# RMSNorm and SiLU over 8192 rows: loads move to ScalarE's queue, stores to SyncE's, and two of four rows are squared on each engine

## The chip, the cores and the metric

The kernel runs on one core of one Trainium2 chip. The metric is device time in microseconds (us), as the median of several executions; one further execution was recorded by the profiler. The engines that matter here are VectorE (DVE in the profile), ScalarE (ACT), SyncE (SP, which here only issues transfers) and the 16 DMA engines that move data between the chip's memory (HBM) and the on-chip buffer (SBUF). A transfer is issued by an instruction on an engine's instruction queue; in the profile ACTq and SPq are the queues of ScalarE and SyncE.

## The reference

```python
batch, seq_len, hidden = 8, 1024, 2048      # x is float32, 67.1 MB
rms = np.sqrt(np.mean(x ** 2, axis=-1, keepdims=True) + eps)
out = gamma * x / rms
return (out * (1 / (1 + np.exp(-out)))).astype(np.float32)
```

Each of the 8192 rows of 2048 numbers is divided by its root mean square, multiplied by gamma, and passed through SiLU. All of x is read once and an output of the same size is written once.

## The kernel before

The rows are cut into 16 blocks of 512 rows. A block is one SBUF tile `xt` of 128 partitions with four rows of 2048 float32 in each (4.194 MB), and it is worked on in place. Six such tiles exist (`BUFS`), so block b uses the tile of block b - 6.

For a block b the work is:

- `load(b)` (line 53): one DMA into the tile, issued on SyncE's queue.
- `sums(b)`: the sum of squares of each of the four rows. VectorE does some rows (line 65), ScalarE the others with a Square that accumulates (line 69). `na` (line 63) is the number of rows for ScalarE: three in blocks 2 to 14, two in the others. Then ScalarE takes the root (line 75), for which it loads another function table, and loads the Silu table back.
- `invert(b)`: VectorE's reciprocal (line 80).
- `finish(b)`: four VectorE instructions (line 85), one for each row, multiply by the reciprocal and by gamma; then ScalarE does one Silu over the whole block (line 89). In the last block (`halves`) the Silu and the store come by halves, two rows each.
- `store(b)` (line 94): one DMA out, issued on ScalarE's queue, followed by the issue of `load(b + 6)` on SyncE's queue, which has to wait until that store has landed, since it overwrites the tile.

The order on each engine is the order of the calls, written out by hand. In the loop (lines 127 to 130) `sums(b + 1)` comes ahead of `finish(b)`. The store of block b - 1 stands behind the first Square of block b + 1 on ScalarE (`after_first`), and that Square waits for block b + 1 to land.

At the start five loads are issued, VectorE fills `ones` by 32 small memsets, gamma comes in by a small DMA on ScalarE's queue into a tile of the same pool (`grow`, line 103), TensorE spreads it over all partitions into PSUM (line 114), and 16 copies (line 117) bring it to SBUF as `g`. The sixth load (line 118) takes the tile that held gamma.

Of the kernel before, what the change touches and what calls it, by code (L numbers as in the profile page):

```python
# [1 line left out]

# [4 lines left out]

ACT = mybir.ActivationFunctionType
ALU = mybir.AluOpType


@with_exitstack
def kernel(
    ctx: ExitStack,
    tc: tile.TileContext,
    x: bass.AP,
    gamma: bass.AP,
    eps: bass.AP,
    out: bass.AP,
):  # L20

    nc = tc.nc
    P = nc.NUM_PARTITIONS
    f32 = mybir.dt.float32
    x2 = x.flatten_outer_dims()  # L30
    o2 = out.flatten_outer_dims()
    n, d = x2.shape
    J = 4
    BUFS, LEAD = 6, 6
    nblk = n // (P * J)
    xb = x2.rearrange("(b p j) d -> b p (j d)", p=P, j=J)
    ob = o2.rearrange("(b p j) d -> b p (j d)", p=P, j=J)

    singles = ctx.enter_context(tc.tile_pool(name="singles", bufs=1))
    pool = ctx.enter_context(tc.tile_pool(name="pool", bufs=BUFS))  # L40
    small = ctx.enter_context(tc.tile_pool(name="small", bufs=2))
    psum = ctx.enter_context(tc.tile_pool(name="psum", bufs=1, space=bass.MemoryType.PSUM))

    g = singles.tile([P, d], f32)
    eps_t = singles.tile([P, 1], f32)
    ones = singles.tile([P, P], f32)
    junk_a = psum.tile([P, d], f32, name="junk_a")
    junk_v = psum.tile([P, d], f32, name="junk_v")
    blocks, rmss, rstds = {}, {}, {}

    def load(b):
        xt = pool.tile([P, J * d], f32, name="xt")
        nc.sync.dma_start(out=xt, in_=xb[b])
        blocks[b] = xt

    def row(b, j):
        return blocks[b][:, j * d:(j + 1) * d]

    def sums(b, after_first=()):


        ss = small.tile([P, J], f32, name="ss")
        na = J - 1 if 2 <= b <= 14 else J // 2
        for j in range(na, J):
            nc.vector.tensor_tensor_reduce(  # L65
                out=junk_v, in0=row(b, j), in1=row(b, j), scale=1.0, scalar=0.0,
                op0=ALU.mult, op1=ALU.add, accum_out=ss[:, j:j + 1])
        for j in range(na):
            nc.scalar.activation(out=junk_a, in_=row(b, j), func=ACT.Square,  # L69
                                 accum_out=ss[:, j:j + 1])  # L70
            if j == 0:
                for s in after_first:
                    store(s)
        rms = small.tile([P, J], f32, name="rms")
        nc.scalar.activation(out=rms, in_=ss, func=ACT.Sqrt, scale=1.0 / d, bias=eps_t)  # L75
        rmss[b] = rms

    def invert(b):
        rstd = small.tile([P, J], f32, name="rstd")
        nc.vector.reciprocal(out=rstd, in_=rmss.pop(b))  # L80
        rstds[b] = rstd

    def finish(b, halves=False):
        for j in range(J):
            nc.vector.scalar_tensor_tensor(out=row(b, j), in0=row(b, j), scalar=rstds[b][:, j:j + 1],  # L85
                                           in1=g, op0=ALU.mult, op1=ALU.mult)
            if j % 2 and (halves or j == J - 1):
                cols = slice((j - 1) * d, (j + 1) * d) if halves else slice(0, J * d)
                nc.scalar.activation(out=blocks[b][:, cols], in_=blocks[b][:, cols], func=ACT.Silu)  # L89
                if halves:  # L90
                    nc.scalar.dma_start(out=ob[b][:, cols], in_=blocks[b][:, cols])

    def store(b):
        nc.scalar.dma_start(out=ob[b], in_=blocks[b])
        if b + LEAD < nblk:
            load(b + LEAD)

    with tc.manual_schedule():


        Q = 4
        w = d // Q
        grow = pool.tile([P, J * d], f32, name="xt")
        for b in range(BUFS - 1):
            load(b)
        for c in range(0, P, 4):
            nc.vector.memset(ones[:, c:c + 4], 1.0)  # L107
        nc.vector.memset(eps_t, float(eps))  # L108
        nc.scalar.activation(out=junk_a[:, 0:1], in_=ones[:, 0:1], func=ACT.Square)  # L109
        nc.scalar.dma_start(out=grow[0:P:P // Q, 0:w],  # L110
                            in_=bass.AP(tensor=gamma.tensor, offset=gamma.offset, ap=[[w, Q], [1, w]]))
        for c in range(Q):
            k = c * (P // Q)
            nc.tensor.matmul(junk_v[:, c * w:(c + 1) * w], ones[k:k + 1, :], grow[k:k + 1, 0:w],  # L114
                             start=True, stop=True)
        for c in range(0, d, P):
            nc.vector.tensor_copy(out=g[:, c:c + P], in_=junk_v[:, c:c + P])  # L117
        load(BUFS - 1)


        last = nblk - 1
        sums(0)
        invert(0)
        finish(0)
        sums(1)
        invert(1)
        for b in range(1, last - 1):
            sums(b + 1, after_first=[b - 1])
            finish(b)
            invert(b + 1)  # L130
        store(last - 2)
        finish(last - 1)
        store(last - 1)
        sums(last)
        invert(last)
        finish(last, halves=True)


# [1 line left out]
_INS = ['x', 'gamma', 'eps']  # L140
_OUTS = [((8, 1024, 2048), 'float32')]

_NUMBERS = {'eps': 9.999999747378752e-06}


# [26 lines left out]
```

## Time and profile before

| what | value |
|---|---|
| three runs | 317.79, 319.18, 319.30 us; median 319.18 |
| profiled execution | 319.30 us, of which the profile's span is 317.5 us |
| busy in the span | VectorE 195.0 us (61%), ScalarE 246.6 us (78%), TensorE 2.1 us |
| moved | 67.12 MB read, 67.11 MB written, 423 GB/s over the span |
| loads | 16 of 4096 KB, median 36.2 us from issue to landing |
| stores | 15 of 4096 KB, median 35.7 us; 2 of 2048 KB, 12.7 us |

Some groups of instructions, each with the mean time of one:

| line, engine | what | count | one, ns |
|---|---|---|---|
| L85 DVE | row times reciprocal times gamma, 128 x 2048 | 64 | 2348 |
| L65 DVE | sum of squares, 128 x 2048 | 19 | 2298 |
| L69 ACT | Square with sum, 128 x 2048 | 45 | 1878 |
| L89 ACT | Silu, 128 x 8192 (15) and 128 x 4096 (2) | 17 | 6628 |
| L75 and L89 ACT | table load | 15 and 15 | 1283 |

Times in the profile are counted from the start of the span. A row of the timeline gives start, duration, engine, line, operation, output and input tile, and in brackets how long the engine was idle ahead of it and what it waited for. A row of the stages gives the stretch and its length, the busy time of each engine, the clock granted to TensorE, the busy share of the DMA engines and their rate. A row of waits gives the waiting instruction, what it waited for, and the total, the count and the longest. The time from issue to landing of a transfer includes what it spends queued behind others.

### The profile page before, as it was taken

The page shows a single profiled execution, that of the slowest core. Times are in us where ns is not written, and L with a number is a line of the kernel's source. Part 1 is how long each engine was busy: PE and PEld are TensorE (multiplying, and loading weights), DVE is VectorE, ACT ScalarE, POOL GpSimd, SP SyncE. Part 2 cuts the span into 40 slices and gives each one's busy share as a digit, 9 for nine tenths or more (in the row PEclk, how much of TensorE's full clock was granted, in tenths as well). Part 3 has the DMA queues.
Part 4 walks back from the last instruction along what each step waited for, and adds up shares of the span by engine and source line. Part 5 has one row for each costly group of instructions (what it writes and reads, how often), then busy time and mean ns, then how long its engine had stood idle before and what let it go on. Part 6 is the DMA issues. An engine that isn't in the chain of part 4 may idle for free.

```text
span 317.5 us, 484 instructions
## 1 busy us (share of the span) xinstructions
PE 2.1 (1%) x8; PEld 0.5 (0%) x8; DVE 195.0 (61%) x167; ACT 246.6 (78%) x155; POOL 0.2 (0%) x4
## 2 busy tenths in 40 slices
PE   0200000000000000000000000000000000000000
PEld 0000000000000000000000000000000000000000
DVE  1679279959493918639094490945819369953800
ACT  1352994999999999997896868968689786797620
POOL 0000000000000000000000000000000000000000
DMA  8999999999999999999999999999999999999994
GB/s 331 409 447 438 421 396 413 446 438 421 442 417 451 409 462 405 454 429 429 446 413 462 396 462 409 450 429 429 442 417 458 400 458 425 433 433 430 447 407 208
DMA packets 4764, 134.26 MB, mean 423 GB/s; under 512 B 532, under 2 KB 532, under 8 KB 536
## 3 DMA queue, kind: packets, MB, share of 16 engines
q1 hardware_dynamic: 2304, 67.11, 49.5%
q10 hardware_dynamic: 2456, 67.12, 49.0%
q14 instruction: 4, 0.03, 0.0%
HBM read 67.12 MB, written 67.11 MB: 423 GB/s over the span
## 4 chain that ended last, share of the span: by engine, by line
DMA 49%; ACT 22%; DVE 17%; issue 7%; DVEq 1%; PE 1%; ACTq 0%; SPq 0%
DMA out_dram<-xt 24%; DMA xt<-in_x_dram 23%; ACT xt L89 14%; DVE xt L85 13%; ACT junk_a L69 4%; DMA xt<-in_gamma_dram 2%; DVE junk_v L65 2%; ACT L75 2%; ACT L89 1%; DVE g L117 1%; DVEq L167 1%; PE junk_v L114 1%; ACT rms L75 0%; DVE rstd L80 0%; DVE ss L65 0%
## 5 line engine op out<-in xcount | busy, mean ns | idle before, releaser
L85 DVE SCALAR_TENSOR_TENSOR xt<-xt,rstd,g 128x2048 f32<-128x2048 f32 x64 | 146.2, 2348 | 0.1
L89 ACT ACTIVATE xt<-xt 128x8192 f32<-128x8192 f32 (+1 forms) x17 | 112.7, 6628 | 36.1 <-DVE xt L85 36.0
L69 ACT ACTIVATE junk_a<-xt 128x2048 f32<-128x2048 f32 x45 | 84.5, 1878 | 18.3 <-DMA xt<-in_x_dram 16.7
L65 DVE CUSTOM_DVE_ANT_0 junk_v<-xt 128x2048 f32<-128x2048 f32 x19 | 43.7, 2298 | 60.9 <-DMA xt<-in_x_dram 60.8
L80 DVE RECIPROCAL rstd<-rms 128x4 f32<-128x4 f32 x16 | 2.8, 175 | 34.6 <-ACT rms L75 34.6
L75 ACT ACT_TABLE_LOAD x15 | 19.2, 1283 | 1.5 <-DVE ss L65 1.3
L89 ACT ACT_TABLE_LOAD x15 | 19.2, 1283 | 0.3
L117 DVE COPY g<-junk_v 128x128 f32<-128x128 f32 x16 | 3.3, 281 | 8.6 <-PE junk_v L114 8.6
L69 ACT ACTIVATION_READ_ACCUMULATOR junk_a<-xt 128x1 f32 x45 | 8.4, 186 | 0.0
L75 ACT ACTIVATE rms<-ss,eps_t 128x4 f32<-128x4 f32 x16 | 4.8, 297 | 0.2
L65 DVE DVE_READ_ACCUMULATOR2_ANT ss<- 128x1 f32 x19 | 2.7, 142 | 0.0
L114 PE MATMUL junk_v<-xt,ones 1*128 1x512 f32 x8 | 2.1, 1132 | 8.2 <-DMA xt<-in_gamma_dram 8.2
L109 ACT ACT_TABLE_LOAD x1 | 1.3, 1283 | 0.7 <-PEq L153 0.7
L107 DVE MEMSET ones<- 128x4 f32 x32 | 0.9, 62 | 0.8 <-PEq L153 0.8
L114 PEld LDWEIGHTS junk_v<-xt,ones 1*128 1x128 f32 x8 | 0.5, 305 | 8.2 <-issue 8.2
L109 ACT ACTIVATE junk_a<-ones 128x1 f32<-128x1 f32 x1 | 0.2, 174 | 0.0
L153 POOL MEMSET const-bfloat16-1.0<- 128x1 bf16 x1 | 0.1, 102 | 0.0
L153 POOL MEMSET const-uint8-127<- 128x1 uint8 x1 | 0.1, 101 | 0.0
L153 POOL MEMSET const-float32-0.0<- 128x1 f32 x1 | 0.1, 99 | 0.2 <-issue 0.2
L153 POOL MEMSET const-float32-1.0<- 128x1 f32 x1 | 0.1, 98 | 0.0
L108 DVE MEMSET eps_t<- 128x1 f32 x1 | 0.1, 59 | 0.0
## 6 DMA issues: line engine op xcount, KB each, us to landing
xt<-in_x_dram SPq DMA_DIRECT2D x16, 4096.0 KB, 36.2
out_dram<-xt ACTq DMA_DIRECT2D x15, 4096.0 KB, 35.7
out_dram<-xt ACTq DMA_DIRECT2D x2, 2048.0 KB, 12.7
xt<-in_gamma_dram ACTq DMA_DIRECT2D x1, 8.0 KB
```

Source lines behind the costliest of these rows:

```text
L65: nc.vector.tensor_tensor_reduce(out=junk_v, in0=row(b, j), in1=row(b, j), scale=1.0, scalar=0.0, op0=ALU.mult, op1=ALU.add, accum_out=ss[ ...
L69: nc.scalar.activation(out=junk_a, in_=row(b, j), func=ACT.Square, accum_out=ss[:, j:j + 1])
L75: nc.scalar.activation(out=rms, in_=ss, func=ACT.Sqrt, scale=1.0 / d, bias=eps_t)
L80: nc.vector.reciprocal(out=rstd, in_=rmss.pop(b))
L85: nc.vector.scalar_tensor_tensor(out=row(b, j), in0=row(b, j), scalar=rstds[b][:, j:j + 1], in1=g, op0=ALU.mult, op1=ALU.mult)
L89: nc.scalar.activation(out=blocks[b][:, cols], in_=blocks[b][:, cols], func=ACT.Silu)
L107: nc.vector.memset(ones[:, c:c + 4], 1.0)
L109: nc.scalar.activation(out=junk_a[:, 0:1], in_=ones[:, 0:1], func=ACT.Square)
L114: nc.tensor.matmul(junk_v[:, c * w:(c + 1) * w], ones[k:k + 1, :], grow[k:k + 1, 0:w], start=True, stop=True)
L117: nc.vector.tensor_copy(out=g[:, c:c + P], in_=junk_v[:, c:c + P])
L153: nc = _bacc.Bacc("TRN2", target_bir_lowering=False, num_devices=1)
L167: with _tile.TileContext(nc) as tc:
```

## The change

- Loads are issued on ScalarE's queue. Six are issued at the very start. In the loop `sums(b + 1)` issues `load(b + 3)` behind its first Square, for blocks 6 to 15; the load still has to wait until the store of block b - 3, which used the tile, has landed.
- Stores are issued on SyncE's queue, directly after `finish(b)` in the program. SyncE has nothing else to issue except gamma's small load.
- `na` is two in every block: each engine takes two rows' squares.
- Silu comes by halves of a block in every block, and not only in the last one. The store is still one for a block, except in the last.
- `ones` is filled by one memset, `g` by one copy of 2048 columns, and gamma's row has a tile of its own, so that all six tiles of the pool are free for blocks from the start.

```diff
-    BUFS, LEAD = 6, 6
+    BUFS = 6
...
+    Q = 4
+    w = d // Q
+    grow = singles.tile([P, w], f32)
...
-        nc.sync.dma_start(out=xt, in_=xb[b])
+        nc.scalar.dma_start(out=xt, in_=xb[b])
...
-        na = J - 1 if 2 <= b <= 14 else J // 2
+        na = J // 2
...
             if j == 0:
                 for s in after_first:
-                    store(s)
+                    load(s)
...
-            if j % 2 and (halves or j == J - 1):
-                cols = slice((j - 1) * d, (j + 1) * d) if halves else slice(0, J * d)
+            if j % 2:
+                cols = slice((j - 1) * d, (j + 1) * d)
                 nc.scalar.activation(out=blocks[b][:, cols], in_=blocks[b][:, cols], func=ACT.Silu)
                 if halves:
-                    nc.scalar.dma_start(out=ob[b][:, cols], in_=blocks[b][:, cols])
+                    nc.sync.dma_start(out=ob[b][:, cols], in_=blocks[b][:, cols])

     def store(b):
-        nc.scalar.dma_start(out=ob[b], in_=blocks[b])
-        if b + LEAD < nblk:
-            load(b + LEAD)
+        nc.sync.dma_start(out=ob[b], in_=blocks[b])
...
-        grow = pool.tile([P, J * d], f32, name="xt")
-        for b in range(BUFS - 1):
+        for b in range(BUFS):
             load(b)
-        for c in range(0, P, 4):
-            nc.vector.memset(ones[:, c:c + 4], 1.0)
+        nc.vector.memset(ones, 1.0)
...
-        nc.scalar.dma_start(out=grow[0:P:P // Q, 0:w],
+        nc.sync.dma_start(out=grow[0:P:P // Q, :],
...
-        for c in range(0, d, P):
-            nc.vector.tensor_copy(out=g[:, c:c + P], in_=junk_v[:, c:c + P])
-        load(BUFS - 1)
+        nc.vector.tensor_copy(out=g, in_=junk_v)
...
         finish(0)
+        store(0)
         sums(1)
         invert(1)
         for b in range(1, last - 1):
-            sums(b + 1, after_first=[b - 1])
+            sums(b + 1, after_first=[b + 3] if BUFS <= b + 3 < nblk else [])
             finish(b)
+            store(b)
             invert(b + 1)
-        store(last - 2)
```

More of the change, by code (lines that the diff above doesn't have):

```diff
@@ L86, in finish @@
                                            in1=g, op0=ALU.mult, op1=ALU.mult)
-            if j % 2 and (halves or j == J - 1):
-                cols = slice((j - 1) * d, (j + 1) * d) if halves else slice(0, J * d)
+            if j % 2:
+                cols = slice((j - 1) * d, (j + 1) * d)
                 nc.scalar.activation(out=blocks[b][:, cols], in_=blocks[b][:, cols], func=ACT.Silu)
                 if halves:
-                    nc.scalar.dma_start(out=ob[b][:, cols], in_=blocks[b][:, cols])
+                    nc.sync.dma_start(out=ob[b][:, cols], in_=blocks[b][:, cols])
     def store(b):
-        nc.scalar.dma_start(out=ob[b], in_=blocks[b])
-        if b + LEAD < nblk:
-            load(b + LEAD)
+        nc.sync.dma_start(out=ob[b], in_=blocks[b])
     with tc.manual_schedule():
-        Q = 4
-        w = d // Q
-        grow = pool.tile([P, J * d], f32, name="xt")
-        for b in range(BUFS - 1):
+        for b in range(BUFS):
             load(b)
-        for c in range(0, P, 4):
-            nc.vector.memset(ones[:, c:c + 4], 1.0)
+        nc.vector.memset(ones, 1.0)
         nc.vector.memset(eps_t, float(eps))
         nc.scalar.activation(out=junk_a[:, 0:1], in_=ones[:, 0:1], func=ACT.Square)
-        nc.scalar.dma_start(out=grow[0:P:P // Q, 0:w],
-                            in_=bass.AP(tensor=gamma.tensor, offset=gamma.offset, ap=[[w, Q], [1, w]]))
+        nc.sync.dma_start(out=grow[0:P:P // Q, :],
+                          in_=bass.AP(tensor=gamma.tensor, offset=gamma.offset, ap=[[w, Q], [1, w]]))
         for c in range(Q):
             k = c * (P // Q)
-            nc.tensor.matmul(junk_v[:, c * w:(c + 1) * w], ones[k:k + 1, :], grow[k:k + 1, 0:w],
+            nc.tensor.matmul(junk_v[:, c * w:(c + 1) * w], ones[k:k + 1, :], grow[k:k + 1, :],
                              start=True, stop=True)
-        for c in range(0, d, P):
-            nc.vector.tensor_copy(out=g[:, c:c + P], in_=junk_v[:, c:c + P])
-        load(BUFS - 1)
+        nc.vector.tensor_copy(out=g, in_=junk_v)
         last = nblk - 1
```

## The prediction, made before the changed kernel was run

> **What bounds the kernel now.** I read the page first, its rows of busy DMA and of the DMA queues.
>
> ```profile
> DMA  8999999999999999999999999999999999999994
> GB/s 331 409 447 438 421 396 413 446 438 421 442 417 451 409 462 405 454 429 429 446 413 462 396 462 409 450 429 429 442 417 458 400 458 425 433 433 430 447 407 208
> ...
> q1 hardware_dynamic: 2304, 67.11, 49.5%
> q10 hardware_dynamic: 2456, 67.12, 49.0%
> ```
>
> The two queues (loads on SyncE's, stores on ScalarE's) together keep the 16 DMA engines busy for 98.5% of the span; VectorE has 61% and ScalarE 78%. Next the same by stage; the last two numbers of a line are the DMA share and GB/s, with a packet counted where it starts.
>
> ```profile
> 1.00:1.50 0.50, 0.00 (x0) 0.00 (x0) 0.50 (x20) 0.50 (x1) 0.00 (x0) 1.00 0.00 0
> 1.50:2.00 0.50, 0.00 (x0) 0.00 (x0) 0.26 (x10) 0.50 (x1) 0.00 (x0) 1.00 2.96 786
> 2.00:12.00 10.00, 2.09 (x8) 0.54 (x8) 1.67 (x9) 0.18 (x2) 0.00 (x0) 1.00 0.91 384
> 12.00:40.00 28.00, 0.00 (x0) 0.00 (x0) 20.25 (x22) 17.37 (x11) 0.00 (x0) 1.00 1.00 431
> 40.00:60.00 20.00, 0.00 (x0) 0.00 (x0) 17.93 (x12) 15.91 (x13) 0.00 (x0) 1.00 1.01 416
> 180.00:220.00 40.00, 0.00 (x0) 0.00 (x0) 24.00 (x17) 32.89 (x23) 0.00 (x0) 1.00 1.00 433
> 300.00:310.00 10.00, 0.00 (x0) 0.00 (x0) 0.08 (x1) 3.62 (x1) 0.00 (x0) 1.00 1.00 428
> 310.00:318.00 8.00, 0.00 (x0) 0.00 (x0) 0.00 (x0) 0.00 (x0) 0.00 (x0) 1.00 0.45 190
> 315.00:316.00 1.00, 0.00 (x0) 0.00 (x0) 0.00 (x0) 0.00 (x0) 0.00 (x0) 1.00 0.04 16
> ```
>
> The rate is the same whether only loads run (12 to 40), both (180 to 220) or only stores (300 to 310). So the span can be written as bytes over rate: 32 blocks of 4.194 MB (16 in, 16 out) at 433 GB/s are 9.69 us each, 310.0 us. The other 7.5 us of the 317.5 us span: 2.2 us missing before 12 (786 GB/s x 0.5 us + 384 x 10 hold 9.8 us of work), 0.8 us in 40 to 60 where the first store begins, 0.4 us at 428 instead of 433 in the last stores, and 4.0 us at the end (8 us at 190 GB/s hold 3.5 us of work, so the mean engine stops at 313.5). Together 7.4. From 315 to 316 a share of 0.04 is left, less than one engine of 16. In the middle there is nothing to win, only something to lose.
>
> The waits then say who gives way to the DMA, and the timeline when.
>
> ```profile
> ACT junk_a L69 <- DMA xt<-in_x_dram: 16.7, 7, 10.9
> ...
> SPq L53 <- DMA out_dram<-xt: 225.3, 10, 54.2
> ```
>
> ```profile
> 217.47 1.88 ACT L69 ACTIVATE junk_a<-xt 128x2048 f32<-128x2048 f32 x1 [0.89 <-DMA xt<-in_x_dram]
> ...
> 220.04 0.33 SPq L53 DMA_DIRECT2D xt<-in_x_dram  x1
> ```
>
> ```profile
> 256.56 1.88 ACT L69 ACTIVATE junk_a<-xt 128x2048 f32<-128x2048 f32 x1 [1.09 <-DMA xt<-in_x_dram]
> 256.62 0.34 ACTq L94 DMA_DIRECT2D out_dram<-xt  x1
> ...
> 303.76 0.34 ACTq L91 DMA_DIRECT2D out_dram<-xt  x1
> ...
> DMA to landing us min/median/max: 12.5/12.7/12.8
> ```
>
> Block 12 lands at 217.5, 13 at 236.9, 14 at 256.6: a period of 19.4 us, which is two blocks at 433 GB/s. A load waits on SyncE's queue until the store of its buffer has landed (225.3 us of waiting that costs nothing there). The last half store is issued at 303.76 and lands at most 12.8 us later, 316.6, though moving its 2.1 MB takes 4.8 us: it stands in a queue. Its last engine ends 3 us behind the mean engine's 313.5.
>
> **The change part by part.** *Squares.* In blocks 2 to 14 one row goes from ScalarE to VectorE: 13 x 2.04 us (first square to second, 236.93 to 238.97) leave ScalarE, 13 x 2.39 us (one sum to the next, 277.20 to 279.59) come to VectorE. *Silu by halves:* 2 x 3.62 in place of 7.03 us, +0.2 us for each of 15 blocks. So ScalarE goes from 246.6 to about 223 us, VectorE from 195 to about 225. Both stay below the 310 us of transfers, which hide them; only their order in a block matters. Counted from a landing: VectorE sums until 4.8, two rows (9.14/4 each) until 9.4, four until 13.9; ScalarE is done with squares and root at 4.8 + 1.28 + 0.31 + 1.28 = 7.7, does its first half at 9.4 and its second at 13.9 to 17.6. Then the store is issued. 17.6 is under 19.4, so the block still waits for its data. If that cover of 1.8 us went, stores would come late, and the queued load would have the engines to itself.
>
> *Start.* 31 memsets and 15 copies less on VectorE; gamma's row gets its own tile, so the sixth load no longer waits for it (it was issued at 10.33). Five loads are 48 us of queued work, so this gives no DMA time. One copy of 2048 columns has no row: at most the 3.26 us that the 16 small ones take, and near the 2.30 us of a sum over as many columns (nearest row; I take it). Either way it ends between 12.6 and 13.6, against the first block's landing at 13.1: a cost of nothing, and if five queued loads did not cover it, half a us.
>
> *Loads on ScalarE.* Sixteen issues of 0.33 to 0.6 us. The first six stand ahead of its first table load and end by 4 us; its data comes at 13.1. Later ones stand behind the first square of block b+1 and wait for the store of block b-3. What is queued behind such a wait: the second square, the root, VectorE's reciprocal, the Silu and with it the next store. Before, that store landed at 220.04, 2.6 us after block 12's landing at 217.47. If nothing moved, ScalarE would stand 2.6 us in each of ten blocks, 0.8 us over its cover. But both times move apart (next part), so I take 0; the upper bound is 10 x 0.8 = 8 us of delayed stores, which the queued load covers.
> [...]
>
> *Is the load queue ever empty?* When block b+1 lands, load b+2 has been queued for a block and is starting; load b+3 comes within 1 us. A load takes 9.7 us alone and 19.4 beside a store. It is never empty, and a full queue alone gives 431 GB/s (12 to 40). So no cost to the end of the loads.
>
> *Stores on SyncE, without the wait for the next landing.* Store 0 was issued at 40.47. Now: data 13.1, sums 17.9, root 19.5, two rows 24.3, four 28.9, second Silu half 32.6: 7.9 us earlier. Store 1: ScalarE's squares of block 1 start at 32.6, root 38.2, VectorE sums of block 2 until 43.2, rows 52.4, Silu 56.0 (was 60.63). Store 0 takes some 20 to 24 us, so the store queue stands empty for 0 to 4 us before store 1. Bytes that stores get earlier, loads get later: both queues have half the rate, so each us that the store queue has work earlier makes the last landing 1 us later. The last load lands 4 to 8 us after the 276.0 of before (256.56 + 19.4), and stores land earlier: ScalarE's 2.6 us of waiting becomes none.
>
> *The end.* This is where something is late. From the landing of block 14 the chain runs: sums 4.8, rows of block 13 until 14.0, of block 14 until 23.2, its second Silu half 26.9, squares of 15 until 30.9, root 32.5, two rows 37.3, Silu and store 41.0, four rows 41.9, Silu 45.5, last store. (Before: 303.76 - 256.56 = 47.2.) Landing at 256.6 + 4 to 8 makes the last issue 306.1 to 310.1. For no gap it must be in hand when the engines end the one before, 313.5 - 4.8 = 308.7, less the time from issue to first bytes, some 1 us (the first load: issued at 0.73, first bytes between 1.5 and 2): 307.7. So between no gap and 2.4 us on the mean engine. The last engine, 3 us behind, sets the end and hides 2.4 of it. Term: 0 to +1 us, I take +0.2.
>
> **The sum:** 317.5 + 0 (engines' work) + 0 (start) + 0 (waits of loads) + 0.2 (end) = 317.7 us span. The profiled execution took 319.30, 1.8 around the span; its time was 0.1 above the median 319.18. Forecast 319.4.
>
> **Rivals.** *The end lies open* (slower). If the stores caught up so far that their queue ran empty in each block, 13 stores and not 12 would be through when the last load lands: (16 + 13) x 9.69 + 3.0 for the start (2.2 + 0.8) = 284.0, plus the 1.3 us by which that landing lags the mean engine now (276.0 against 313.5 - 4 x 9.69 = 274.7) and some tenths: 285.6. Block 14 then lands at 266.2, the last store is issued at 311.7 with the engines idle, and needs s + 4.8 us to its end, 0.3 to its semaphore and 0.9 to the span's end (317.5 - 316.6). s is 1 us by the first load, and at most 4 if an idle queue answers like a busy one (store 0, issued at 40.47, takes 64.90 - 40.47 = 24.4 us to its landing, which SyncE's next load, issued at 64.90, waits for; 19.4 beside a load leave 5, 1 of them for the landing): span 318.7 to 321.7, time 320.5 to 323.5, middle 322. It decides, by more than the measurement can tell, from a last issue at 312 with s = 1, or 309 with s = 4. For it: stores go out first now, and there is 2 to 5 us less work behind the last one. Against: stores arrive every 19.4 us and need 19.4 us each, so a backlog once formed (stores 2 and 3 come some 14 us apart, while data is at hand) stays.
>
> *The load queue runs dry, or ScalarE stands at a load* (slower). Some 4 us of idle DMA in each of ten blocks: 360 us. Against it stands the whole block that is always queued; it decides only if an issue comes more than 9.7 us late.
>
> *The end gets shorter* (faster). If the last engine's 3 us went (2.5 of them, say), 317.5 - 2.5 = 315.0, time 316.8. For it: fewer instructions to fetch (the profile has few packets for them); against: nothing in the change touches that engine.
>
> *It does not do what it says.* The store of before waits 1.1 us for a landing (idle ahead of 256.56) and the load 2.6: freeing both may move no block at all. The time would be the forecast's, 319.3.
>
> **How the numbers follow.** Forecast, with the last rival in it: 0.68. Open end 0.16, dry queue 0.06, shorter end 0.10. A measurement of this kernel can tell about 0.5%, 1.6 us, from no change. The forecast's own range is 318.0 to 320.8; to leave out no more than 2 in 10 it reaches down to 317.5 and up to the open end's middle, 322.0. Faster 0.10, same 0.68, slower 0.22.
>
> **What would show it.** DMA share 1.00 and about 433 GB/s in every stage from 12 to 300; ScalarE waiting for block data, not for stores; first store near 32.6; last block landing at 280 to 284, last issue 306 to 310. A DMA share under 0.95 between the last landing and 310, or a wait of ScalarE's queue on a store in most blocks, would prove me wrong.

## The result

| | median of 6 runs | lowest to highest | profiled execution | its span |
|---|---|---|---|---|
| before | 318.92 us | 317.79 to 319.30 | 319.30 us | 317.5 us |
| changed | 317.23 us | 317.16 to 317.56 | 317.26 us | 315.1 us |

The ratio is 0.9951, with a 95% interval of 0.9935 to 0.9967: the changed kernel is faster by half a per cent, 1.7 us. That is below the 317.5 us at which the predicted range began.

### The profile after

The page of the changed kernel, its DMA row and the queues (packets, MB, share of 16 engines):

```profile
DMA  8999999999999999999999999999999999999997
...
q10 hardware_dynamic: 2304, 67.11, 49.8%
q1 hardware_dynamic: 2456, 67.12, 49.4%
q14 instruction: 2, 0.02, 0.0%
```

Queue 10 (ScalarE's) now carries the loads and queue 1 (SyncE's) the stores, and the engines are full as before (the two together 99.2% of the span; before 98.5%). The third queue is named instruction, and its packets are read here as the program's code: the runs below have 2 to 4 of them, 2 in the changed kernel and 4 in the same kernel with 184 small instructions more. Its row on the page of before, which the prediction did not show:

```profile
q14 instruction: 4, 0.03, 0.0%
```

By stage (the last two numbers are DMA share and GB/s), the changed kernel:

```profile
180.00:220.00 40.00, 0.00 (x0) 0.00 (x0) 27.60 (x18) 28.43 (x19) 0.00 (x0) 1.00 1.01 435
...
276.00:300.00 24.00, 0.00 (x0) 0.00 (x0) 19.37 (x12) 18.30 (x11) 0.00 (x0) 1.00 1.01 434
300.00:310.00 10.00, 0.00 (x0) 0.00 (x0) 1.24 (x1) 3.98 (x2) 0.00 (x0) 1.00 0.95 408
310.00:318.00 8.00, 0.00 (x0) 0.00 (x0) 0.00 (x0) 0.00 (x0) 0.00 (x0) 1.00 0.40 170
```

The middle runs at 435 GB/s where it ran at 433. The 0.95 from 300 to 310 follows 1.01 in the 24 us ahead of it, since a packet is counted where it starts; it is no gap, as the last half stores show, which stand queued (below). From 310 on 3.1 us of work are left (8 us at 170 GB/s) instead of 3.5. The rest of the difference one sees only us by us. The changed kernel:

```profile
312.00:313.00 1.00, 0.00 (x0) 0.00 (x0) 0.00 (x0) 0.00 (x0) 0.00 (x0) 1.00 0.99 426
313.00:314.00 1.00, 0.00 (x0) 0.00 (x0) 0.00 (x0) 0.00 (x0) 0.00 (x0) 1.00 0.12 49
314.00:315.00 1.00, 0.00 (x0) 0.00 (x0) 0.00 (x0) 0.00 (x0) 0.00 (x0) 1.00 0.00 0
```

The kernel before, in the same stretches (its next one, 315 to 316, stands in the prediction with a share of 0.04):

```profile
312.00:313.00 1.00, 0.00 (x0) 0.00 (x0) 0.00 (x0) 0.00 (x0) 0.00 (x0) 1.00 0.92 393
313.00:314.00 1.00, 0.00 (x0) 0.00 (x0) 0.00 (x0) 0.00 (x0) 0.00 (x0) 1.00 0.39 164
314.00:315.00 1.00, 0.00 (x0) 0.00 (x0) 0.00 (x0) 0.00 (x0) 0.00 (x0) 1.00 0.08 33
```

From 312 on, the mean engine has 1.43 us of packets in the kernel before (0.92 + 0.39 + 0.08 + 0.04) and 1.11 us in the changed one: 0.3 us less. But the span is 2.4 us shorter. 16 GB/s in one us are 16 KB: one packet, on one engine out of 16. So before, fifteen engines had all but ended by 314 and one still moved its last packets until past 316; now all end within a us of each other. Nearly all of the difference between the two profiled executions is that one late engine.

The waits of the changed kernel, the two that the prediction named:

```profile
SPq L96 <- ACT xt L91: 267.3, 15, 22.6
```

```profile
ACT junk_a L71 <- DMA xt<-in_x_dram: 26.2, 11, 7.9
```

A store on SyncE's queue now waits for Silu, not for the next landing, and ScalarE waits for its block, not for stores. The timeline at one block:

```profile
201.46 1.88 ACT L71 ACTIVATE junk_a<-xt 128x2048 f32<-128x2048 f32 x1 [1.85 <-DMA xt<-in_x_dram]
201.47 0.33 ACTq L55 DMA_DIRECT2D xt<-in_x_dram  x1
```

The load goes out 0.01 us after the square starts, so its buffer was free. And the end: block 14's first square, the issue of the two last half stores (merged, 4.86 us from the first issue to the end of the second, which was issued at 304.91), and their time to landing.

```profile
259.55 1.88 ACT L71 ACTIVATE junk_a<-xt 128x2048 f32<-128x2048 f32 x1 [1.87 <-DMA xt<-in_x_dram]
...
300.39 4.86 SPq L93 DMA_DIRECT2D out_dram<-xt  x2
...
DMA to landing us min/median/max: 9.0/9.0/9.0
```

9.0 us for a half that needs 4.8 alone (2.1 MB at 433 GB/s): it still waits in the queue for the half ahead of it, and the engines have no gap.

### The profile page after: what moved, and what is told of

It reads as the page before. It is cut to its first block, busy times and chain, and to the rows that moved or that the text cites. A ratio compares the mean times of both kernels' runs of the same rounds, so it can differ in the third digit from the quotient of the medians.

```text
span 315.1 us, 438 instructions
## 1 busy us (share of the span) xinstructions
PE 2.1 (1%) x8; PEld 0.5 (0%) x8; DVE 223.6 (71%) x147; ACT 223.7 (71%) x144; POOL 0.2 (0%) x4
## 4 chain that ended last, share of the span: by engine, by line
DMA 65%; DVE 18%; ACT 10%; issue 2%; DVEq 1%; ACTq 0%
DMA xt<-in_x_dram 65%; DVE xt L87 13%; ACT xt L91 6%; DVE junk_v L67 4%; ACT junk_a L71 2%; ACT L77 2%; DVEq L161 1%; ACT L91 0%; ACT rms L77 0%; DVE rstd L82 0%; DVE ss L67 0%; DVEq L67 0%; ACTq L77 0%
## 5 line engine op out<-in xcount | busy, mean ns | idle before, releaser
L91 ACT ACTIVATE xt<-xt 128x4096 f32<-128x4096 f32 x32 | 115.5, 3616 | 39.2 <-DVE xt L87 39.2
L67 DVE CUSTOM_DVE_ANT_0 junk_v<-xt 128x2048 f32<-128x2048 f32 x32 | 73.6, 2299 | 56.6 <-DMA xt<-in_x_dram 55.9
L71 ACT ACTIVATE junk_a<-xt 128x2048 f32<-128x2048 f32 x32 | 60.1, 1879 | 26.7 <-DMA xt<-in_x_dram 26.2
L111 DVE COPY g<-junk_v 128x2048 f32<-128x2048 f32 x1 | 2.3, 2292 | 9.3 <-PE junk_v L109 9.3
L71 ACT ACTIVATION_READ_ACCUMULATOR junk_a<-xt 128x1 f32 x32 | 6.0, 186 | 0.0
L67 DVE DVE_READ_ACCUMULATOR2_ANT ss<- 128x1 f32 x32 | 4.5, 141 | 0.0
L109 PE MATMUL junk_v<-grow,ones 1*128 1x512 f32 x8 | 2.1, 1132 | 8.1 <-DMA grow<-in_gamma_dram 8.1
```

Source lines behind the costliest of these rows:

```text
L67: nc.vector.tensor_tensor_reduce(out=junk_v, in0=row(b, j), in1=row(b, j), scale=1.0, scalar=0.0, op0=ALU.mult, op1=ALU.add, accum_out=ss[ ...
L111: nc.vector.tensor_copy(out=g, in_=junk_v)
```

## The experiments

Theory F: one DMA engine ended late because code packets set it back, and the changed kernel has fewer instructions (438 in its profile, 484 before), so fewer such packets. On VectorE the short start takes 46 away and the squares bring 26, 147 busy instructions for 167; on ScalarE it is 144 for 155. The rivals: Q, the exchange of the queues; B, the balance of the rows; T or W, the moment of the first store or VectorE's time. Ratios are to the kernel before in the same comparison, with 95% intervals. The number of code packets is from each page.

### Are the queues or the rows the cause?

The changed kernel with its loads on SyncE and its stores on ScalarE:

```diff
-        nc.scalar.dma_start(out=xt, in_=xb[b])
+        nc.sync.dma_start(out=xt, in_=xb[b])
...
-        nc.sync.dma_start(out=ob[b], in_=blocks[b])
+        nc.scalar.dma_start(out=ob[b], in_=blocks[b])
...
```

The last half stores and gamma's small load change places in the same way.

> The changed kernel with the queues as before: loads and gamma's place exchanged, loads on SyncE, stores on ScalarE directly after their Silu. Theory F: the same number of instructions, 2 packets of code, span 314.9 to 315.6, ratio 0.994 to 0.997. Theory Q: the gain goes, span 317 to 318, ratio 0.999 to 1.001.

317.42 us, ratio 0.9956 (0.9944 to 0.9967), span 315.6, 3 code packets where 2 were expected, the third only at 309 us. The gain stays: Q falls.

The kernel before with `na = J // 2` in all blocks:

> The kernel before with two rows squared on each engine in every block: 26 instructions fewer on ScalarE, 26 more on VectorE. Theory F: ScalarE's late packet of code goes (its total falls under the place where the second was fetched), VectorE's stays and comes earlier: 3 packets, the late engine is the one that brings VectorE's code, span 316.8 to 317.6, ratio 0.998 to 1.000. A third theory, B (the balance of the rows made the gain): span 315 to 315.6, ratio 0.995.

318.65 us, ratio 0.9996 (0.9984 to 1.0007), 3 code packets. B falls: two rows on each engine alone bring nothing. Theory F had it so: this VectorE has the long start and 26 instructions more.

### Is it the code?

The kernel before with the short start:

```diff
-        for c in range(0, P, 4):
-            nc.vector.memset(ones[:, c:c + 4], 1.0)
+        nc.vector.memset(ones, 1.0)
...
-        for c in range(0, d, P):
-            nc.vector.tensor_copy(out=g[:, c:c + P], in_=junk_v[:, c:c + P])
+        nc.vector.tensor_copy(out=g, in_=junk_v)
```

> The kernel before with one memset and one copy at the start: 46 VectorE instructions fewer, nothing else. Theory F (code fetches): the 2.4 us that the span lost came from one DMA engine that ended late, since it also brought in code (page of before: 4 packets on the queue named instruction; of the changed kernel: 2). With 46 instructions fewer VectorE needs one packet less: 3 on that queue, none near 296 us, last half store lands within 11.5 us of its issue (before 12.8), span 315.3 to 316.3, ratio 0.994 to 0.997. Theory Q (the exchange of the queues and the earlier stores shorten the end): 4 or 3 packets, last landing 12.8 as before, span 317 to 318, ratio 0.999 to 1.001.

A plain miss: 321.41 us (319.29 to 323.54), ratio 1.0066 (1.0037 to 1.0096), although there were 3 code packets, as expected. Something else that costs more came in; the next part looks for it.

The reverse, the changed kernel with the long start of before:

> The changed kernel with the 32 memsets and 16 copies of before: 46 VectorE instructions more. Theory F: one packet of code more (3), again in the last 40 us, one DMA engine behind the others by 1 to 2.4 us: span 316 to 317.5, ratio to before 0.997 to 1.000. Theory Q: 315.1 as the changed kernel, ratio 0.995.

318.38 us, ratio 0.9985 (0.9976 to 0.9993), span 316.3, 3 code packets. Two thirds of the gain are gone (0.9985 - 0.9951 = 0.0034 of 0.0049). This moves the start by half a us too (first store at 33.2 for 32.7), so the next four runs add instructions in the middle, where VectorE or ScalarE waits for data.

```diff
             invert(b + 1)
+            if b in (6, 7):
+                for _ in range(23):
+                    nc.vector.memset(pad, 1.0)
```

> The changed kernel with 46 small memsets of an unused tile on VectorE in blocks 6 and 7 (23 each, where VectorE waits for data anyway). Theory F (a packet of code sets its DMA engine back by 0.5 to 0.9 us, and the engine with most of them ends last): 3 code packets for 2, span 315.5 to 316.2, ratio to before 0.996 to 0.998. Rival T (it was the moment of the first store, not the code, that cost the time in the run with the long start): nothing else moves, span 315.1, ratio 0.995.

318.04 us, ratio 0.9965 (0.9952 to 0.9978), span 316.3, 3 code packets. That gives back less than a third of the gain (0.0014 of 0.0049), and the interval overlaps that of the changed kernel (0.9935 to 0.9967), so this run alone decides little. With `b in range(4, 12)`:

> The same with 184 memsets, 23 in each of blocks 4 to 11. Theory F: 4 code packets, three of them VectorE's, on one DMA engine: span 316.0 to 317.0, ratio 0.9975 to 1.0005. Rival T: 315.1, ratio 0.995.

319.01 us, ratio 0.9993 (0.9985 to 1.0002), span 317.0, 4 code packets. The changed kernel has lost its gain, by nothing but 184 small memsets (11.4 us busy) in time that VectorE spent waiting; T falls. Its page and its last us:

```profile
q14 instruction: 4, 0.03, 0.0%
```

```profile
314.00:315.00 1.00, 0.00 (x0) 0.00 (x0) 0.00 (x0) 0.00 (x0) 0.00 (x0) 1.00 0.04 16
315.00:316.00 1.00, 0.00 (x0) 0.00 (x0) 0.00 (x0) 0.00 (x0) 0.00 (x0) 1.00 0.04 16
```

The single late engine is back. The control spends almost as much busy time on VectorE with 8 instructions instead of 184:

```diff
             invert(b + 1)
+            if b in range(4, 12):
+                nc.vector.memset(junk_v[:, 0:1350], 1.0)
```

> The changed kernel with 8 long memsets of unused PSUM space on VectorE, one in each of blocks 4 to 11, of the same 1.4 us as the 23 small ones of the run with 184. Theory F (it is the packets of code): 2 packets, span 315.0 to 315.6, ratio 0.994 to 0.996. Rival W (it is VectorE's time in these blocks): as with 184 small ones, span 316.5 to 317.2, ratio 0.998 to 1.000.

317.42 us, ratio 0.9952 (0.9940 to 0.9964), span 315.3, 2 code packets. They were 1183 ns each, 9.5 us in all against 11.4. The page and the last us:

```profile
q14 instruction: 2, 0.02, 0.0%
```

```profile
313.00:314.00 1.00, 0.00 (x0) 0.00 (x0) 0.00 (x0) 0.00 (x0) 0.00 (x0) 1.00 0.12 49
314.00:315.00 1.00, 0.00 (x0) 0.00 (x0) 0.00 (x0) 0.00 (x0) 0.00 (x0) 1.00 0.00 0
```

No late engine. The control is not quite equal: VectorE also stands idle for 11.8 us ahead of the small memsets, for 2.2 ahead of the long ones. But VectorE still waits for its blocks in both (34.3 us with the small ones, 44.5 with the long ones, 55.9 in the changed kernel), so W falls: it is the number of instructions.

The loads show the delay as it comes, since each is issued when a block has landed. With the small memsets load 7 goes out at 85.33 us and load 8 at 105.31 (with the long ones 85.40 and 104.77); load 11 at 163.36 and load 12 at 183.50 (162.85 and 182.22). So the landings fall back by about 0.6 us and then by 0.8 more. The first two code packets of the run with small memsets come at 89.6 and 90.5 us, its third at 165.3. Not every packet shows: the control's two, at 90.5 and 110.1, leave its landings 19.4 us apart. For ScalarE:

```diff
             store(b)
+            if b in (5, 6, 7):
+                for _ in range(8):
+                    nc.scalar.activation(out=junk_a[:, 0:1], in_=ones[:, 0:1], func=ACT.Square)
```

> The changed kernel with 24 one-column squares on ScalarE, 8 in each of blocks 5 to 7 where it waits for data. Theory F, for any engine: ScalarE goes over the place of its second packet (195 in the kernels that had it), 3 code packets, span 315.6 to 316.4, ratio 0.9965 to 0.9985. Rival V (only VectorE's packets cost, as the short start at the same moment suggests, which kept two of ScalarE's and took 317.17 us): 3 packets, span 315.0 to 315.4, ratio 0.994 to 0.996.

317.24 us, ratio 0.9943 (0.9930 to 0.9956), span 315.6, 3 code packets. F fails for ScalarE, and V holds: its second packet, at 270 us, costs nothing that can be measured. Read packet by packet, the traces suggest why. A code packet of 8 KB takes 0.31 us. The data packet right behind one of VectorE's takes mostly 1.56 to 1.78 us instead of 1.21, behind one of ScalarE's mostly 1.32 to 1.33. So two of ScalarE's (0.8 to 0.9 us) would set an engine back hardly more than one of VectorE's (0.7 to 0.9), and two of VectorE's on the same DMA engine would add up. The trace names neither the DMA engine of a packet nor the engine whose code it is (that is judged by how many instructions each had run), so this is argued, not shown.

### The moment of the first stores

Why was the short start slow? It brought the first store from 40.47 to 39.84 us. The same kernel with a copy that fills that time:

```diff
         nc.vector.tensor_copy(out=g, in_=junk_v)
+        nc.vector.tensor_copy(out=g[:, 0:860], in_=junk_v[:, 0:860])
```

> The kernel before with one memset and one copy, and one more copy of 860 columns, which fills the 0.6 us that the short start had saved (that kernel took 321.41 us). 45 instructions fewer than before, the same moment of the first stores (40.5, 60.6). Theory S and F: the long packets of the short start go, and with them its loss; VectorE's second code packet is gone too: 3 code packets, span 316.0 to 317.0, ratio 0.995 to 0.999. Rival (the short start costs time for a reason of its own): span 319 to 322, ratio 1.004 to 1.010.

317.17 us (316.99 to 318.08), ratio 0.9948 (0.9934 to 0.9962), 3 code packets. One instruction brings back 4.2 us. This is the kernel before, its queues, rows and Silu untouched, with 45 instructions fewer, and it has the whole gain of the change. Its five runs lie in two groups, three at 317.0 to 317.2 and two at 318.1, the profiled one among these; so here too something small still moves the time by 1 us. Two more fillings, of 430 and of 1720 columns:

> The kernel before with the short start and a copy of 430 columns: first stores some 0.1 to 0.2 us later than with the short start alone (321.41 us), 0.4 us earlier than with 860 columns (317.17 us). Theory S (the moment of the first stores against the turns of 1.21 us decides): a time between, 317 to 322 us, wide from run to run, the long packets again between 60 and 260 us if it is slow. Rival (chance of a run): 317 to 318 us.

> The same with 1720 columns: first stores about 0.9 us later than with 860. Theory S: 1.5 us after the slow one, more than a turn of 1.21 us, so it may be slow again: 317 to 322 us. Rival (only an early start is slow): 317.0 to 318.2 us.

| columns filled | first store issued, us | time, us | lowest to highest | ratio |
|---|---|---|---|---|
| 0 | 39.84 | 321.41 | 319.29 to 323.54 | 1.0066 (1.0037 to 1.0096) |
| 430 | 40.03 | 319.95 | 318.82 to 321.59 | 1.0025 (1.0010 to 1.0041) |
| 860 | 40.40 | 317.17 | 316.99 to 318.08 | 0.9948 (0.9934 to 0.9962) |
| 1720 | 41.37 | 317.76 | 317.27 to 318.16 | 0.9960 (0.9948 to 0.9972) |

Not chance: 0.4 us earlier costs 2.8 us, 0.6 us earlier 4.2; 1.0 us later costs little (0.6 us, and the intervals overlap). The slow one loses it in the middle, as this stretch of 80 us shows, first for 0 columns:

```profile
140.00:220.00 80.00, 0.00 (x0) 0.00 (x0) 45.76 (x28) 63.65 (x40) 0.00 (x0) 1.00 1.00 425
```

and then for 860:

```profile
140.00:220.00 80.00, 0.00 (x0) 0.00 (x0) 47.70 (x31) 66.61 (x44) 0.00 (x0) 1.00 1.00 433
```

The engines are full in both (share 1.00) but move 425 GB/s instead of 433: the 32 KB packets of the loads take 1.26 us in the mean instead of 1.21, those of the stores 1.21 in both. In the last us of the kernel with 0 columns the share falls in steps, and half is left where the other kernels have ended:

```profile
315.00:316.00 1.00, 0.00 (x0) 0.00 (x0) 0.00 (x0) 0.00 (x0) 0.00 (x0) 1.00 0.54 229
316.00:317.00 1.00, 0.00 (x0) 0.00 (x0) 0.00 (x0) 0.00 (x0) 0.00 (x0) 1.00 0.50 213
```

Does the changed kernel have such a moment? Its first store held back:

```diff
         finish(0)
-        store(0)
         sums(1)
+        c = blocks[0][:, 0:3072]
+        nc.vector.scalar_tensor_tensor(out=c, in0=c, scalar=ones[:, 0:1], in1=c,
+                                       op0=ALU.mult, op1=ALU.max)
+        store(0)
         invert(1)
```

> The changed kernel with the first store held back by about 4.6 us: VectorE rewrites 3072 columns of block 0 with their own values ahead of it, in its idle time. Store 0 then ends (58.6 to 59.3 instead of 54.0 to 54.7) just when store 1, issued at 55.8, gets its first packet through (59.3). Theory S (DMA engines get out of step when a store comes to hand just while the one before it ends; some take it up a turn earlier than others, and packets then take longer than 1.21 us): DMA rate between 60 and 260 under 433, engines apart by 2 to 4 us at the end, span 316.5 to 320. Rival: where the engines are full, a moment is nothing: span 315.0 to 315.5.

318.02 us (317.55 to 320.13), ratio 0.9973 (0.9958 to 0.9989), 2 code packets; the first store was issued at 36.87 for 32.69. Slower than the changed kernel by 0.2% (the intervals overlap), and two of twelve runs at 320.1; the profiled one (span 315.9) shows no loss of rate in the middle. So a moment may matter here too, but less than theory S said, and not in the way it said.

**What stays open.** Why packets take longer after some first stores. Engines out of step (theory S) are not shown: the first 16 packets of a store in the middle start 2.4 us and more apart in the slow profile (0 columns), and 0.5 to 1.1 us apart in that of before, but 1.7 and 2.0 in the fast ones of 860 and 1720 columns.

Nor is it shown why the kernel before pays more for its code. With 46 instructions added, in the middle or at the start, the changed kernel has by the same judgement two of VectorE's packets, as many as the kernel before, yet it gives back only 0.0014 and 0.0034 of its gain of 0.0049; the kernel before gains 0.0052 by losing one. Silu by halves, and the load's place behind the landing, were not tried alone.

## Why the prediction was right or wrong

*What bounds the kernel: right.* 310.0 us of transfers at 433 GB/s, and the engines full from 12 to 310 in both kernels. That ScalarE's and VectorE's work was free held as well (223.7 and 223.6 us busy, predicted 223 and 225).

*Loads on ScalarE: right.* No wait on a store: none stands among ScalarE's waits. The engines stay at 433 to 436 GB/s from 60 to 260 us, so the load queue did not run dry.

*Stores earlier: right in the first stores, mis-sized behind.* Store 0 at 32.69 (predicted 32.6), store 1 at 55.77 (56.0). Block 14 came 259.55 - 256.56 = 3.0 us later, not 4 to 8.

*The end: the chain right, its effect nil.* From block 14 to the last issue 304.91 - 259.55 = 45.4 us (45.5). With the smaller delay the last issue came before the 306.1 of the range, and before the 307.7 at which a gap would open. So no rest of 0.2 us.

*Wrong: two steps, about the same engine.* "Start" put 31 memsets and 15 copies less at "a cost of nothing", because it priced only their time on VectorE. And "The end" carried the last DMA engine's 3 us behind the others over as fixed: its term was +0.2 us where -2.4 us was measured on the span (317.5 to 315.1 in the profiled executions; -1.7 us on the median times). The lag went. The rival with a shorter end named the right cause, "fewer instructions to fetch", but was set at 0.10, against it that "nothing in the change touches that engine". The instructions did touch it: with 184 more, in time that VectorE only waited, the changed kernel went from 0.9951 to 0.9993 and the late engine came back; with 46 more at the start it went to 0.9985; and with 45 fewer at the same moment the kernel before went to 0.9948. That rival's 316.8 us was near the 317.23 measured. The row that hinted at it was on the page: 4 packets of code. How many us each packet costs was not settled by the runs.

*The baseline: 0.3 us.* The forecast was built on the median of three runs, 319.18; the median of six was 318.92. That is a small part of the miss.

By these runs the code is not free in this kernel, whose DMA engines are full (99.2% of the span): the run with 184 small instructions took 319.01 us and the one with 8 long ones 317.42, 0.4% more by the ratios (0.9993 and 0.9952), 0.5% by the times.

## What to carry to other kernels

In this kernel, whose DMA engines are full, the end was set by the last of the 16, not by their mean: the span fell by 2.4 us while the mean engine had 0.3 us less to move from 312 on. So look at the last us one by one, and at every queue on the page, however small its share. Small instructions cost time here, as it seems by their code, even on an engine that only waited: 184 on VectorE took the changed kernel from 317.23 to 319.01 us, 24 on ScalarE did not slow it (317.24). And try a change of half a per cent again with the start shifted by a few tenths of a us, for 0.56 us of it alone moved the kernel before by 4.2 us (321.41 to 317.17).

## What the runs showed of the hardware that was not expected

- The packets that are read as code are 8 KB and take 0.31 us each, and the data packet right behind one took mostly 1.32 to 1.78 us instead of 1.21, so they seem to share the DMA engines with the data. In the run with 184 memsets those taken for VectorE's came when it had run 54, 180 and 320 instructions, 126 and 140 apart.
- Two kernels whose first store differs by 0.56 us (39.84 and 40.40) differ by 4.2 us, with the engines busy all the time in both: 425 against 433 GB/s from 140 to 220 us.
- A store and a load in turn run at 433 to 436 GB/s (60 to 260 us, kernel before and changed), as fast as loads alone (431 to 434 from 12 to 40 us in the kernels whose first store comes later), and it made no difference that could be measured which of the two queues carried which (0.9951 and 0.9956).
